# Encoder layer on one core: the convolution group normalised two tiles a unit, two attention pairs' values a unit later, and a first transfer of 656 columns

## The chip, the cores and the metric

One core of a Trainium2 chip runs the whole layer; the other cores are unused. The metric is device time in microseconds (us). TensorE (PE) multiplies matrices, VectorE (DVE) and ScalarE (ACT) do elementwise work, GpSimd (POOL) and SyncE (SP) here mostly issue DMAs.

## The reference, cut to what matters

512 positions, 2048 channels, float32. The change lies in the first half of the layer, up to the shared output projection.

```python
xn = rms_norm(x, attn_norm_g[l])
proj = jnp.einsum("bsd,dc->bsc", xn, w_in[l])
u_val, u_gate, q, k, v = jnp.split(proj, split_pts, axis=-1)
y_conv = conformer_conv(u_val, u_gate, ...)   # GLU, depthwise conv of 31, layer_norm over 1024 channels, silu
y_na = neighborhood_attention(heads(q), heads(k), heads(v), rpb[l])
mixed = concat([rms_norm(y_conv, conv_out_g[l]), rms_norm(y_na, na_out_g[l])])
x = x + jnp.einsum("bsc,cd->bsd", mixed, w_out[l])
# then a gated MLP with a depthwise conv of 3, and a last rms_norm
```

## The kernel before

**Units.** Channels lie on the partitions, positions along the free axis. Every product is taken in two parts for precision: an operand is split into a rounded part and the rest (`whi`, `wlo` for weights; `xh`, `xl` for the input; `mah`, `mal` for the normalised convolution group; `mbh`, `mbl` for the attention group). A *unit* is one weight tile of 128x1024: DMA to `raw`, ACT rounds it to `whi` (L129), DVE subtracts to `wlo` (L130), and `group` (L142) issues 24 matmuls of 128x512: sixteen with `whi`, alternately on L146 and L147, then eight with `wlo` on L149. Four `whi` and four `wlo` tiles exist (`NW = 4`), so the `whi` of a unit can be written once the unit four before it has used its own.

**The order.** `ORDER` (L63) sets the projections: `a` is a convolution tile (gate and value), `V` the values, `q` one pair of heads (a q projection of two units and a k projection of two). After the projections `out_half` (L676) multiplies the convolution group (`ma`) by its half of the output weights, one unit for each of 16 output tiles `po`, then the attention group (`mb`). After each unit `tick` (L154) runs the next step of two generators: `attention` (L542) and, on its own list, `group_a` (L493). What a generator emits between two `yield`s so falls behind one unit; each engine then works its own queue in order.

**Attention.** For each pair of heads one step emits the value products of the pair before (`values`, `po<-pt,v` on L608), the scores (`sc<-k,q`, L562) and the softmax. Three units later (four for pairs 5 and 6, `LATER`) the probabilities are transposed on PE (`trp`, L588) and ACT copies them out of PSUM as `pt` (L597); the next step's `values` needs these copies.

**The convolution group.** `group_a` waits for the last tap, sums the eight `y` tiles, subtracts the mean, squares, takes the root `rln` in `roots_of_sums` (L271), and then, for eight tiles at a stretch: multiply by `rln` (DVE, L517), Silu (ACT, L518) and `split` (L208), which makes `mah` on ACT (L211) and `mal` on DVE (L212). The squares of all eight tiles (ACT L217 and L220, sums on DVE L221) stand behind that, with no `yield` in the stretch. `RA_AFTER` yields later the second root `ra` is taken; `read_a` (L691) needs it before it can read an output tile of the first half out of PSUM (`oa<-po,ra`, L696).

**PSUM.** The pool `psm` has three banks of 128x512, used in turn by each q or k projection `pj`, by one half of each `values`, and by each output tile `po`. A bank is free again when its reader is done: DVE's `q<-pj` or `k<-pj` (L536), DVE's `ao` addition (L617), or DVE's `oa<-po,ra`. The column sums `st` use the bank of the other half of `values`.

**The start.** Eight matmuls on ones (`WARM`, L117) run while the first data come. The input comes in four rows of 512 columns, each with 384 columns of weights for the first three projections and 16 of gains, in one transfer `xw` (L318). For row 0 ACT and DVE split x (L328, L330, L333) and the weights (L329 the first 128 columns, L331 the other 256); the first matmuls are on L455.

Of the kernel before, what the change touches and what calls it, by code (L numbers as in the profile page):

```python
# [10 lines left out]
F32 = mybir.dt.float32  # L11
F32R = mybir.dt.float32r
AF = mybir.ActivationFunctionType
ALU = mybir.AluOpType
AX = mybir.AxisListType

P = 128
D = 2048
S = 512
# [11 lines left out]
KD = D // P  # L31
NC_ = CONV // P
# [15 lines left out]
AHEAD = 3  # L48
FAR = 8
NW = 4  # L50
WARM = 8
ROWS = 4
SOONER = 100
TAPS = 4
# [7 lines left out]
ROW = 2048  # L62
ORDER = "aaaaaaVVaqaqqqqqqq"  # L63
LATER = (5, 6)
RA_AFTER = 5

PCOLS = [("g1", KD), ("dww", NC_ * CK), ("dwb", NC_), ("lng", NC_), ("lnb", NC_), ("cog", NC_),
         ("nag", NC_), ("g2", KD), ("fww", 2 * NF * 3), ("fwb", 2 * NF)]
# [9 lines left out]
def layer(ctx: ExitStack, tc: tile.TileContext, xT, xg, xn, xw, w_0, w_in, w_v, w_out, w_up, w_down, par, tab, g3, out):  # L78
    nc = tc.nc
# [16 lines left out]
    def t2(name, dt=F32):  # L96
        return tp.tile([P, S], dt, tag="t2k", name=name)

    def t4(shape, name):

        return wpool.tile(shape, F32, tag="raw", name=name, bufs=NR)

    prm = consts.tile([P, NPAR], F32, name="prm")
    g1 = consts.tile([P, KD], F32, name="g1")

    def pc(name, i):
        o = POFF[name] + i
        return prm[:, o:o + 1]
# [6 lines left out]
    ps = psm.tile([P, S], F32, tag="mm", name="warm")  # L115
    for _ in range(WARM):
        nc.tensor.matmul(ps[:, :P], ones, ones, start=True, stop=True)  # L117
# [3 lines left out]
    def raw_unit(src, n):  # L121
        raw = t4([P, U * P], "raw")
        return raw, nc.sync.dma_start(raw[:, :n], src)
# [81 lines left out]
        if job:  # L205
            open_job.append(job)

    def split(src, g, name):  # L208

        h, l = t2(name + "h", F32R), t2(name + "l", F32R)  # L210
        nc.scalar.activation(h, src, AF.Copy, scale=g)  # L211
        nc.vector.scalar_tensor_tensor(l, src, g, h.bitcast(F32), op0=ALU.mult, op1=ALU.subtract)  # L212
        return h, l

    def sum_sq(acc, src, first, to=slice(0, S)):
        if first:
            nc.scalar.activation(acc, src, AF.Square)  # L217
        else:
            q = t2("sq")[:, to]
            nc.scalar.activation(q, src, AF.Square)  # L220
            nc.vector.tensor_add(acc, acc, q)  # L221
# [35 lines left out]
    def halved(src):  # L257

        h, l = t2("ah", F32R), t2("al", F32R)
        nc.scalar.activation(h, src, AF.Copy)  # L260
        nc.vector.tensor_sub(l, src, h.bitcast(F32))
        return h, l

    def column_sums(two):

        ps = stat()
        for i in range(2):
            nc.tensor.matmul(ps, ones_r, two[i], start=i == 0, stop=i == 1)
        return ps

    def roots_of_sums(acc, n, name, wait=1):  # L271

# [12 lines left out]

    xs, x1 = [], []
    pin = tc.keep_in_program_order

    def split_x(k, x, g=None):
        h, l = t2("xh", F32R), t2("xl", F32R)  # L290
        g = (g1 if g is None else g)[:, k:k + 1]
        pin(nc.scalar.activation(h, x, AF.Copy, scale=g))
        pin(nc.vector.scalar_tensor_tensor(l, x, g, h.bitcast(F32), op0=ALU.mult, op1=ALU.subtract))
        xs.append((h, l))
# [18 lines left out]
    todo = [(t, i) for t in range(S // P) for i in range(2)]  # L313
    for k in range(ROWS):
        n = 3 * P
        both = t4([P, S + n + KD], "xw")
        m = S + n + (0 if k else KD)
        pin(nc.sync.dma_start(both[:, :m], xw[k][:, :m]))  # L318
        x, raw, lo = both[:, :S], both[:, S:S + n], t2("wel", F32R)[:, :n]
        if k:  # L320
            split_x(k, x)
            his = [t2("weh", F32R)[:, :n]]
            pin(nc.scalar.activation(his[0], raw, AF.Copy))
        else:
            his = [t2("weh", F32R)[:, :P], t2("weh", F32R)[:, P:n]]
            h, l = t2("xh", F32R), t2("xl", F32R)
            g = both[:, S + n:S + n + 1]
            pin(nc.scalar.activation(h[:, :H], x[:, :H], AF.Copy, scale=g))  # L328
            pin(nc.vector.tensor_copy(his[0], raw[:, :P]))  # L329
            pin(nc.vector.tensor_scalar(h[:, H:], x[:, H:], g, None, op0=ALU.mult))  # L330
            pin(nc.scalar.activation(his[1], raw[:, P:], AF.Copy))  # L331
            pin(nc.vector.tensor_copy(g1, both[:, S + n:]))
            pin(nc.vector.scalar_tensor_tensor(l, x, g, h.bitcast(F32), op0=ALU.mult, op1=ALU.subtract))  # L333
            xs.append((h, l))
        o = 0
        for h in his:
            to = slice(o, o + h.shape[-1])
            pin(nc.vector.tensor_sub(lo[:, to], raw[:, to], h.bitcast(F32)))
            o = to.stop
        pieces.append((k, k + 1, his, lo))  # L340
    for p in range(ROWS // 2, KD // 2):
        x = t4([P, 2 * S], "x")
# [6 lines left out]
    for u in range(2):  # L349
        raw, i = raw_unit(w_in[1, :, u * U * P:(u + 1) * U * P], U * P)  # L350
# [8 lines left out]
    for step in ORDER:  # L359
# [5 lines left out]
        i = next(a_ if step == "a" else q_)  # L365
# [69 lines left out]
    ys, ypair, gate = [], [], []  # L435
# [55 lines left out]
    ma, ra = [], []  # L491

    def group_a():  # L493
        yield
        while taps:
            yield
        acc = t2("acc")
        nc.vector.tensor_add(acc, ys[0], ys[1])
        for i in range(2, NC_):
            nc.vector.tensor_add(acc, acc, ys[i])  # L500
        two = halved(acc)
        yield
        yield
        ps = column_sums(two)
        mu = t2("mu")
        nc.vector.tensor_scalar(mu, ps, 1.0 / CONV, None, op0=ALU.mult)
        acc = t2("acc")
        for i in range(NC_):
            nc.vector.tensor_sub(ys[i], ys[i], mu)
            sum_sq(acc, ys[i], i == 0)  # L510
        yield
        yield
        yield
        r = yield from roots_of_sums(acc, CONV, "rln")
        acc = t2("acc")
        for i in range(NC_):
            nc.vector.tensor_mul(ys[i], ys[i], r)  # L517
            nc.scalar.activation(ys[i], ys[i], AF.Silu, scale=pc("lng", i), bias=pc("lnb", i))  # L518
            ma.append(split(ys[i], pc("cog", i), "ma"))
        for i in range(NC_):  # L520
            sum_sq(acc, ys[i], i == 0)
        for _ in range(RA_AFTER):
            yield

        ra.append((yield from roots_of_sums(acc, CONV, "ra")))

# [15 lines left out]
    def attention():  # L542


        def banks(name):
            two = psa.tile([P, 2, S], F32, tag="sc", name=name)
            return [two[:, j, :2 * SLOTS] for j in range(2)] + [
                psa.tile([P, 2 * SLOTS], F32, tag="tr", name=name, bufs=2) for _ in range(2)]
# [65 lines left out]
        def taken(p, po):  # L614
            ao = t2("ao")
            nc.scalar.activation(grid(ao), blocks(po[0]), AF.Copy)
            nc.vector.tensor_add(grid(ao), grid(ao), blocks(po[1]))  # L617
            mb.append(split(ao, pc("nag", p), "mb"))
            sum_sq(acc_na, ao, p == 0)

        pts = None
        for p in range(NP_ + 1):
            while len(qks) < min(p + 1, NP_):
                yield
            if p < NP_:
                tabs = [t4([P, 2, 2 * SLOTS], "tab") for _ in QUADS]
                for n, tb in enumerate(tabs):
                    nc.sync.dma_start(tb, tab[2 * p:2 * p + 2, :, n * 2 * SLOTS:(n + 1) * 2 * SLOTS]
                                      .rearrange("h p k -> p h k"))
            yield  # L630
            if p:
                po = [psa.tile([P, S], F32, tag="po", name="po"), psm.tile([P, S], F32, tag="mm", name="po")]
                values(p - 1, pts, po)
            if p < NP_:
                four = banks("sc")
                for n, quad in enumerate(QUADS):
                    scores(*qks[p], quad, four[2 * n:][:2], p or n)
            if p:
                taken(p - 1, po)
            if p == NP_:  # L640
                return
# [426 lines left out]
    a = four(True)  # L1068
# [30 lines left out]
def _cols(a):  # L1099

    return np.asarray(a).reshape(-1, P).T
# [70 lines left out]
```

## Time and profile before

| | us |
|---|---|
| runs of the kernel, median of 3 | 1961.98 (1961.77 to 1962.09) |
| the profiled execution | 1962.36 |
| its span, first to last instruction | 1960.4 |
| PE busy in the span | 1938.6 |
| DVE busy in the span | 1611.0 |
| ACT busy in the span | 1083.8 |

In the rows below, a line of the timeline gives start, duration, engine, line of the kernel, operation, what it writes and reads, and in brackets the idle time of the engine ahead of it with what ended that. A row with "x8" stands for eight instructions in a row, and its duration runs from the first's start to the last's end. PEclk is the granted TensorE clock as a share of full speed.

### The profile page before, as it was taken

Reading aid. Unit: us, or ns where it says so; the run is one execution under the profiler, and the core shown is the slowest. Engines: PE = TensorE matmul, PEld = TensorE weight load, DVE = VectorE, ACT = ScalarE, POOL = GpSimd, SP = SyncE. Lnnn points to the kernel's source line nnn. Section 1 sums busy time; section 2 is a strip of 40 time slices with the busy share of each in tenths; the row PEclk is TensorE's granted clock in tenths of the full one; section 3 lists DMA queues with packets and bytes.
Section 4 is the critical chain, followed back from the end, with each engine's and each line's share of the span. In section 5 each row is a group of like instructions: output and inputs, shape, how many; then the busy total and the mean of one; then the engine's idle time right before and its main releaser. Section 6 shows DMA issues by size and latency. Waiting matters only on the chain.

```text
span 1960.4 us, 27992 instructions
## 1 busy us (share of the span) xinstructions
PE 1938.6 (99%) x10327; PEld 1652.5 (84%) x10327; DVE 1611.0 (82%) x2310; ACT 1083.8 (55%) x1725; POOL 226.3 (12%) x310
## 2 busy tenths in 40 slices
PE   9999999979999999999999999999999999999998
PEld 8888888868888888888888888888888888888886
DVE  5999878975657898888888888888889898885764
ACT  7222233576526666666666666666666644554654
POOL 0111111100011111111111111111110300000000
PEclk9999999999999999999999999999999999999999
DMA  9676667767758899999999999999995967666553
GB/s 372 179 194 178 190 182 189 194 167 218 251 151 215 212 250 253 270 243 271 241 270 244 270 247 265 262 249 263 249 257 166 386 239 236 216 215 194 192 201 121
DMA packets 141529, 448.89 MB, mean 229 GB/s; under 512 B 14928, under 2 KB 27216, under 8 KB 139984
## 3 DMA queue, kind: packets, MB, share of 16 engines
q1 hardware_dynamic: 89168, 291.90, 43.1%
q0 software_dynamic: 42624, 148.92, 35.1%
q10 hardware_dynamic: 9600, 6.29, 1.1%
q8 instruction: 81, 1.33, 0.3%
q14 instruction: 56, 0.46, 0.1%
HBM read 428.17 MB, written 111.15 MB: 275 GB/s over the span
## 4 chain that ended last, share of the span: by engine, by line
PE 97%; ACT 1%; DVE 1%; issue 0%; ACTq 0%
PE pu L823 44%; PE pd L962 21%; PE pj L146 5%; PE pj L147 5%; PE pj L149 5%; PE pv L417 4%; PE po L146 3%; PE po L147 3%; PE po L149 3%; PE pj L455 1%; PE po L608 1%; PE pj L459 1%; PE sc L562 1%; PE trp L588 0%; PE trx L718 0%; ACT y L518 0%
## 5 line engine op out<-in xcount | busy, mean ns | idle before, releaser
L129 ACT ACTIVATE whi<-raw 128x1024 fp32r<-128x1024 f32 (+1 forms) x574 | 604.1, 1055 | 550.6 <-PE pd L962 116.0
L130 DVE TENSOR_TENSOR wlo<-raw,whi 128x1024 fp32r<-128x1024 f32 (+1 forms) x574 | 698.6, 1218 | 214.8 <-ACT whi L129 186.5
L823 PE MATMUL pu<-xc,whi 128*128 128x512 f32 x2464 | 593.1, 391 | 0.0
L823 PEld LDWEIGHTS pu<-xc,whi 128*128 128x128 f32 x2464 | 451.4, 188 | 86.8 <-DVE xc L711 0.4
L823 PEld LDWEIGHTS pu<-xc,wlo 128*128 128x128 f32 x2464 | 319.4, 191 | 13.7
L823 PE MATMUL pu<-xc,wlo 128*128 128x256 f32 x2464 | 324.3, 283 | 0.0
L962 PE MATMUL pd<-whi,ho 128*128 128x512 f32 x1232 | 305.1, 389 | 0.0
L962 PEld LDWEIGHTS pd<-whi,ho 128*128 128x128 f32 x1232 | 231.1, 188 | 48.7 <-DVE vl L836 0.5
L146 PE MATMUL pj<-xh,whi 128*128 128x512 f32 x464 | 182.0, 392 | 0.0
L485 DVE SCALAR_TENSOR_TENSOR y<-ch,prm,y 128x500 f32<-128x500 f32 (+14 forms) x240 | 176.9, 741 | 5.4
L147 PE MATMUL pj<-xl,whi 128*128 128x512 f32 x464 | 180.6, 389 | 0.0
L962 PE MATMUL pd<-wlo,ho 128*128 128x512 f32 x616 | 165.1, 389 | 0.0
L962 PEld LDWEIGHTS pd<-wlo,ho 128*128 128x128 f32 x616 | 115.6, 188 | 24.0
L832 ACT ACTIVATE pu<-pu 128x512 f32<-128x512 f32 x132 | 76.6, 580 | 92.0 <-PE pu L823 92.0
L772 POOL DMA_DIRECT2D raw<-in_w_up x88 | 78.6, 893 | 351.5 <-DVE wlo L130 160.8
L203 POOL DMA_DIRECT2D ws<-in_w_down x88 | 79.9, 907 | 316.7 <-DMA ws<-in_w_down 126.5
L149 PE MATMUL pj<-xh,wlo 128*128 128x512 f32 x464 | 114.6, 389 | 0.0
L146 PEld LDWEIGHTS pj<-xh,whi 128*128 128x128 f32 x464 | 87.1, 188 | 19.5 <-issue 1.6
L149 PEld LDWEIGHTS pj<-xh,wlo 128*128 128x128 f32 x464 | 87.1, 188 | 18.1
L147 PEld LDWEIGHTS pj<-xl,whi 128*128 128x128 f32 x464 | 87.1, 188 | 17.8
L200 POOL DMA_DIRECT2D ws<-ws x44 | 23.3, 530 | 317.5 <-PE pj L149 102.9
L200 POOL DMA_DIRECT2D ws<-in_w_down x44 | 23.4, 531 | 298.5 <-PE pj L149 125.9
(215 smaller groups left out, 2109.2 us busy)
## 6 DMA issues: line engine op xcount, KB each, us to landing
raw<-in_w_up SPq DMA_DIRECT2D x220, 512.0 KB, 5.9
ws<-in_w_down POOLq DMA_DIRECT2D x132, 512.0 KB, 6.5
raw<-in_w_up POOLq DMA_DIRECT2D x88, 512.0 KB, 7.4
raw<-ws SPq DMA_DIRECT2D x88, 512.0 KB, 3.3
raw<-in_w_down SPq DMA_DIRECT2D x66, 512.0 KB, 3.8
raw<-in_w_in SPq DMA_DIRECT2D x58, 512.0 KB, 5.3
ws<-ws POOLq DMA_DIRECT2D x44, 512.0 KB, 5.5
raw<-in_w_out SPq DMA_DIRECT2D x32, 512.0 KB, 4.9
```

The lines of the kernel that those rows point to most:

```text
L129: i = nc.scalar.activation(hi[:, :n], raw[:, :n], AF.Copy)
L130: j = nc.vector.tensor_sub(lo[:, :n], raw[:, :n], hi[:, :n].bitcast(F32))
L146: nc.tensor.matmul(ps, hi, mh, start=first and k == 0, stop=False)
L147: nc.tensor.matmul(ps, hi, ml, start=False, stop=False)
L149: i = nc.tensor.matmul(ps, lo[:, wk * P:(wk + 1) * P], mh, start=False, stop=last and k == len(ws) - 1)
L203: nc.gpsimd.dma_start(wsum[c][k], w_down[k, {1: A21, 2: A11, 4: A11, 6: A12}[c]], accum_op=ALU.add, max_dma_last_dim=ROW)
L417: m = nc.tensor.matmul(banks[c], xs[2 * u + k][x][:, c * P:(c + 1) * P], w[l][:, k * S:(k + 1) * S], start=u == x == l == k == 0, stop=las ...
L485: nc.vector.scalar_tensor_tensor(y[:, a:b], h[:, a + j - PAD:b + j - PAD], prm[:, o:o + 1], y[:, a:b], op0=ALU.mult, op1=ALU.add)
L772: nc.gpsimd.dma_start(a[c], w_up[f, q2], accum_op=ALU.add)
L823: i = nc.tensor.matmul(ps[:, :n], part[:, k * P:(k + 1) * P], comb[c][k][:, :n], start=j == 0 and not more, stop=j == 2 * U - 1, skip_grou ...
L832: nc.scalar.activation(to, ps, AF.Copy)
L962: m = nc.tensor.matmul(ps[i], h[:, o + t * P:o + (t + 1) * P], w[:, d], start=start and not more and kind == 0 and j == 0, stop=stop and k ...
```

## The change

- `group_a`: a `yield` after every third tile in the loop that subtracts the mean (one of three plain yields behind it stays). In the loop of the normalisation each tile's square follows its split at once, a `yield` stands after every second tile, and the `RA_AFTER` yields are gone. So the eight tiles fall behind four units.
- `split(..., vector=True)`: for the convolution group the rounded part `mah` is made on DVE (a `tensor_scalar`) and no longer on ACT.
- `SLOW = (4, 5)`: one more `yield` ahead of the step that holds the values of pairs 4 and 5. Since the generator goes on from there, everything of the attention behind it moves one unit, then two.
- The start: the first transfer holds x, 128 columns of weights and the gains (656 columns); the other 256 weight columns of row 0 go to a tile `wer` by a second transfer. Rows 1 to 3 are transferred as before. `WARM` is 7.

```diff
-WARM = 8
+WARM = 7
-RA_AFTER = 5
+SLOW = (4, 5)
...
-    def split(src, g, name):
+    def split(src, g, name, vector=False):
...
-        nc.scalar.activation(h, src, AF.Copy, scale=g)
+        if vector:
+            nc.vector.tensor_scalar(h, src, g, None, op0=ALU.mult)
+        else:
+            nc.scalar.activation(h, src, AF.Copy, scale=g)
         nc.vector.scalar_tensor_tensor(l, src, g, h.bitcast(F32), op0=ALU.mult, op1=ALU.subtract)
...
-        both = t4([P, S + n + KD], "xw")
-        m = S + n + (0 if k else KD)
+        both = t4([P, S + n], "xw")
+        m = S + (n if k else P + KD)
         pin(nc.sync.dma_start(both[:, :m], xw[k][:, :m]))
...
         else:
+            raw = [both[:, S:S + P], t2("wer")[:, :n - P]]
+            pin(nc.sync.dma_start(raw[1], xw[k][:, m:]))
             his = [t2("weh", F32R)[:, :P], t2("weh", F32R)[:, P:n]]
...
         for i in range(NC_):
             nc.vector.tensor_sub(ys[i], ys[i], mu)
             sum_sq(acc, ys[i], i == 0)
-        yield
-        yield
+            if i % 3 == 2:
+                yield
         yield
         r = yield from roots_of_sums(acc, CONV, "rln")
         acc = t2("acc")
         for i in range(NC_):
             nc.vector.tensor_mul(ys[i], ys[i], r)
             nc.scalar.activation(ys[i], ys[i], AF.Silu, scale=pc("lng", i), bias=pc("lnb", i))
-            ma.append(split(ys[i], pc("cog", i), "ma"))
-        for i in range(NC_):
+            ma.append(split(ys[i], pc("cog", i), "ma", True))
             sum_sq(acc, ys[i], i == 0)
-        for _ in range(RA_AFTER):
-            yield
+            if i % 2 == 1:
+                yield
...
             while len(qks) < min(p + 1, NP_):
+                yield
+            if p - 1 in SLOW:
                 yield
```

What this does to ACT's queue behind the root `rln`, where the copies `pt` of pair 4 (counted from 0) stand. Before:

```order
L281 ACTIVATE r<-rln 128x512 x2
L518 ACT_TABLE_LOAD
L518 ACTIVATE y<-y,prm 128x512 x2
L211 ACTIVATE mah<-y,prm 128x512
L518 ACTIVATE y<-y,prm 128x512
L211 ACTIVATE mah<-y,prm 128x512
L518 ACTIVATE y<-y,prm 128x512
L211 ACTIVATE mah<-y,prm 128x512
L518 ACTIVATE y<-y,prm 128x512
L211 ACTIVATE mah<-y,prm 128x512
```

```order
L211 ACTIVATE mah<-y,prm 128x512 x2
L217 ACTIVATE acc<-y 128x512
L220 ACTIVATE sq<-y 128x512 x7
L597 ACTIVATE pt<-trp 128x384 x4
L129 ACTIVATE whi<-raw 128x1024 x2
L616 ACTIVATE ao<-po 128x8x8x8
```

Now, in the numbers of the changed file's lines (Silu L523, squares L220 and L223, `pt` L601):

```order
L523 ACT_TABLE_LOAD
L523 ACTIVATE y<-y,prm 128x512 x3
L220 ACTIVATE acc<-y 128x512
L523 ACTIVATE y<-y,prm 128x512 x2
L223 ACTIVATE sq<-y 128x512
L601 ACTIVATE pt<-trp 128x384 x4
L129 ACTIVATE whi<-raw 128x1024
L223 ACTIVATE sq<-y 128x512
L523 ACTIVATE y<-y,prm 128x512
L129 ACTIVATE whi<-raw 128x1024 x2
L223 ACTIVATE sq<-y 128x512
L523 ACTIVATE y<-y,prm 128x512 x2
```

Ahead of `pt` stood eight Silus, eight `mah` and eight squares; now five Silus and two squares, and no `mah`.

DVE's queue behind `rln`, up to the reads of PSUM that free PE's banks. Before:

```order
L283 TENSOR_SCALAR rln<-r,rln 128x512
L517 TENSOR_TENSOR y<-y,rln 128x512 x8
L212 TENSOR_SCALAR mal<-y,prm,mah 128x512 x8
L221 TENSOR_TENSOR acc<-acc,sq 128x512 x4
L536 TENSOR_TENSOR k<-pj,rstd_545 128x512
L221 TENSOR_TENSOR acc<-acc,sq 128x512 x3
L130 TENSOR_TENSOR wlo<-raw,whi 128x1024 x2
L617 TENSOR_TENSOR ao<-ao,po 128x8x8x8
```

Now, the end of the same stretch (`mah` L212, `mal` L215, sums of squares L224, reads of q and k L540, `ao` L621):

```order
L130 TENSOR_TENSOR wlo<-raw,whi 128x1024
L224 TENSOR_TENSOR acc<-acc,sq 128x512
L212 TENSOR_SCALAR mah<-y,prm 128x512
L130 TENSOR_TENSOR wlo<-raw,whi 128x1024
L215 TENSOR_SCALAR mal<-y,prm,mah 128x512
L224 TENSOR_TENSOR acc<-acc,sq 128x512
L212 TENSOR_SCALAR mah<-y,prm 128x512
L215 TENSOR_SCALAR mal<-y,prm,mah 128x512
L224 TENSOR_TENSOR acc<-acc,sq 128x512
L540 TENSOR_TENSOR q<-pj,rstd_546 128x512
L621 TENSOR_TENSOR ao<-ao,po 128x8x8x8
```

From `rln` to `q<-pj` DVE now has eight `y`, six `mah`, six `mal`, five sums `acc`, `k<-pj`, three `wlo` and `q<-pj`; the last two tiles' `mah` and `mal` follow behind the next scores. On PE two units, where there was one, now stand between the transposes and the value products of pair 4, and again for pair 5, where the second of them is the first unit of the output projection.

More of the change, by code (lines that the diff above doesn't have):

```diff
@@ L315, in layer @@
         n = 3 * P
-        both = t4([P, S + n + KD], "xw")
-        m = S + n + (0 if k else KD)
+        both = t4([P, S + n], "xw")
+        m = S + (n if k else P + KD)
         pin(nc.sync.dma_start(both[:, :m], xw[k][:, :m]))
-        x, raw, lo = both[:, :S], both[:, S:S + n], t2("wel", F32R)[:, :n]
+        x, raw, lo = both[:, :S], [both[:, S:m]], t2("wel", F32R)[:, :n]
         if k:
@@ L322, in layer @@
             his = [t2("weh", F32R)[:, :n]]
-            pin(nc.scalar.activation(his[0], raw, AF.Copy))
+            pin(nc.scalar.activation(his[0], raw[0], AF.Copy))
         else:
+            raw = [both[:, S:S + P], t2("wer")[:, :n - P]]
+            pin(nc.sync.dma_start(raw[1], xw[k][:, m:]))
             his = [t2("weh", F32R)[:, :P], t2("weh", F32R)[:, P:n]]
             h, l = t2("xh", F32R), t2("xl", F32R)
-            g = both[:, S + n:S + n + 1]
+            g = both[:, S + P:S + P + 1]
             pin(nc.scalar.activation(h[:, :H], x[:, :H], AF.Copy, scale=g))
-            pin(nc.vector.tensor_copy(his[0], raw[:, :P]))
+            pin(nc.vector.tensor_copy(his[0], raw[0]))
             pin(nc.vector.tensor_scalar(h[:, H:], x[:, H:], g, None, op0=ALU.mult))
-            pin(nc.scalar.activation(his[1], raw[:, P:], AF.Copy))
-            pin(nc.vector.tensor_copy(g1, both[:, S + n:]))
+            pin(nc.scalar.activation(his[1], raw[1], AF.Copy))
+            pin(nc.vector.tensor_copy(g1, both[:, S + P:m]))
             pin(nc.vector.scalar_tensor_tensor(l, x, g, h.bitcast(F32), op0=ALU.mult, op1=ALU.subtract))
@@ L335, in layer @@
         o = 0
-        for h in his:
+        for r, h in zip(raw, his):
             to = slice(o, o + h.shape[-1])
-            pin(nc.vector.tensor_sub(lo[:, to], raw[:, to], h.bitcast(F32)))
+            pin(nc.vector.tensor_sub(lo[:, to], r, h.bitcast(F32)))
             o = to.stop
@@ L1121 @@
     w_0 = np.ascontiguousarray(np.stack([w_in[i].reshape(P, KD, P) for i in (NC_, 0, NC_ + 1)], 2)).reshape(P, -1)
-    xw = np.stack([np.concatenate([xg[k // 2][:, k % 2 * S:(k % 2 + 1) * S], w_0[:, 3 * k * P:3 * (k + 1) * P],
-                                   _cols(a["attn_norm_g"][0])], axis=1) for k in range(ROWS)])
+    xw = []
+    for k in range(ROWS):
+        w, g = w_0[:, 3 * k * P:3 * (k + 1) * P], _cols(a["attn_norm_g"][0])
+        xw.append(np.concatenate([xg[k // 2][:, k % 2 * S:(k % 2 + 1) * S]]
+                                 + ([w, g] if k else [w[:, :P], g, w[:, P:]]), axis=1))
+    xw = np.stack(xw)
     wo = a["w_out"][0]
```

## The prediction

> **What bounds the kernel now.** I read the page first, then who waited for whom on PE, then the timeline round the one long wait.
>
> ```profile
> span 1960.4 us, 27992 instructions
> PE 1938.6 (99%) x10327; PEld 1652.5 (84%) x10327; DVE 1611.0 (82%) x2310; ACT 1083.8 (55%) x1725; POOL 226.3 (12%) x310
> PE 97%; ACT 1%; DVE 1%; issue 0%; ACTq 0%
> PE po L608 <- ACT pt L597: 12.7, 1, 12.7
> PE warm L117 <- DVE ones L112: 1.1, 1, 1.1
> 1939.94 12.47 PE pd L962 x54
> ```
>
> PE is 97% of the chain that ended last. In the whole span it waits twice: 1.1 us at the start, and once 12.7 us for ACT's `pt`. Its last matmul in the chain ends at 1952.4, 8.0 before the span's end: 1.1 + 12.7 + 8.0 is all of 1960.4 - 1938.6. So only what shortens that wait, the start, or adds a new PE wait, can move the time. ACT's timeline there:
>
> ```profile
> 426.25 1.52 ACT L518 ACTIVATE y<-y,prm 128x512 f32<-128x512 f32 x2 [0.91 <-DVE y L517]
> 427.68 0.71 ACT L211 ACTIVATE mah<-y,prm 128x512 fp32r<-128x512 f32 x1
> 435.59 1.32 ACT L211 ACTIVATE mah<-y,prm 128x512 fp32r<-128x512 f32 x2
> 437.33 3.73 ACT L220 ACTIVATE sq<-y 128x512 f32<-128x512 f32 x7
> 440.97 1.59 ACT L597 ACTIVATE pt<-trp 128x384 f32<-128x384 f32 x4
> 442.45 2.00 ACT L129 ACTIVATE whi<-raw 128x1024 fp32r<-128x1024 f32 x2
> ```
>
> PE had left the transposes by 424.21 (next rows), but ACT first worked through Silu, `mah` and squares of eight tiles, from 426.25 to 440.97. PE's timeline, its chain, and two windows:
>
> ```profile
> 424.21 0.48 PE L146 MATMUL pj<-xh,whi 128*128 128x512 f32 x1
> 442.61 2.62 PE L608 MATMUL po<-pt,v 64*64 64x64 f32 x48 [12.70 <-ACT pt L597]
> 452.66 0.39 PE L146 MATMUL pj<-xh,whi 128*128 128x512 f32 x1
> 456.45 1.81 PE pj L149 x8
> 461.89 1.81 PE pj L149 x8
> 475.92 1.37 PE po L608 x38
> 478.65 0.43 PE pj L146
> 442.60:446.00 3.40, 3.39 (x64) 3.17 (x66) 3.30 (x4) 2.45 (x3) 0.00 (x0) 0.50 0.78 271
> 458.00:470.00 12.00, 12.00 (x60) 10.04 (x59) 4.18 (x4) 3.13 (x6) 2.17 (x3) 1.00 0.73 199
> ```
>
> A unit is 461.89 - 456.45 = 5.44 us; values and scores without a wait are 478.65 - 475.92 = 2.73 us. After the wait the granted clock is 0.50 (the last but two number of a window's row) and the same values and scores take 447.1 - 442.6 = 4.5. From the unit that begins at 424.21 to the one at 452.66 lie unit, values and scores, unit: 5.44 + 2.73 + 5.44 = 13.61, and they took 28.45. **The stall is worth 14.8 us**, 12.7 of waiting and some 2 of slow rows.
>
> **The change part by part.** *The old wait.* PE now has the unit at 424.2 and one more, so it reaches the values at 424.21 + 10.88 = 435.1. ACT starts at 426.25 (DVE's `y` sets that, unchanged). Five Silus at 0.70 apart (two take 1.52 with 0.1 of overlap), two squares at 0.53 (3.73 for seven) and the four copies, 1.5, end at 426.25 + 3.5 + 1.1 + 1.5 = 432.4. `pt` is 2.7 us early: all 14.8 us go, unless something else is late.
>
> *What is late next: DVE.* PE continues with values and scores to 437.8 and a unit to 424.21 + 3 x 5.44 + 2.73 = 443.3. The unit behind that writes the PSUM bank of the last q projection, and `q<-pj` stands at the end of DVE's row of the change. DVE's prices:
>
> ```profile
> 425.53 4.90 DVE L517 TENSOR_TENSOR y<-y,rln 128x512 f32<-128x512 f32 x8
> 430.35 2.78 DVE L212 SCALAR_TENSOR_TENSOR mal<-y,prm,mah 128x512 fp32r<-128x512 f32 x4
> 443.76 2.35 DVE L130 TENSOR_TENSOR wlo<-raw,whi 128x1024 fp32r<-128x1024 f32 x2
> L996 DVE TENSOR_SCALAR g<-g 128x512 f32<-128x512 f32 x2 | 0.8, 422 | 1.0 <-DMA g<-in_g 1.0
> L483 DVE TENSOR_SCALAR y<-ch,prm 128x512 f32<-128x512 f32 x8 | 4.3, 541 | 0.0
> ```
>
> Start to start, a two-tensor operation of 512 takes 0.60 (eight `y` from 425.53 to 430.35), `mal` 0.68, a `wlo` 1.14. From 425.53: eight `y` 4.8, six `mal` 4.1, five sums 3.0, `k` and `q` 1.2, three `wlo` 3.4, together 16.5. No row has `mah` on DVE: between L996, whose scalar is a constant, and L483, with two scalars from a tile; less 0.07 that neighbours overlap, 0.35 to 0.47. I take 0.43; the upper bound is a two-tensor price, 0.60. Six are 2.6 (2.1 to 3.6), so `q` is read at 425.5 + 19.1 = 444.6 and **PE waits 1.4 us** (0.9 to 2.4). Behind `q<-pj` on DVE stand `ao` and the next softmax, which ACT's exponentials wait for.
>
> [...]
>
> *The second root.* `ra` is now taken earlier: its column sum `st<-ah` stands inside a unit, behind fifteen matmuls, in the third unit after 444.65. PE gets there at 444.65 + 10.88 + 15 x 0.227 = 458.9. ACT makes `ah` behind the softmax of pair 5, the last squares and two `whi`:
>
> ```profile
> 446.03 0.68 DVE L617 TENSOR_TENSOR ao<-ao,po 128x512 f32<-128x512 f32 x1
> 451.56 0.68 DVE L536 TENSOR_TENSOR q<-pj,rstd 128x512 f32<-128x512 f32 x1
> 487.19 1.48 ACT L580 ACTIVATE s<-s,su 128x192 f32<-128x192 f32 x4
> L577 ACT ACTIVATE s<-s,nm 128x192 f32<-128x192 f32 x64 | 28.3, 442 | 14.8 <-DVE nm L574 14.8
> 538.86 0.63 ACT L260 ACTIVATE ah<-accna 128x512 fp32r<-128x512 f32 x1 [0.90 <-DVE accna L221]
> ```
>
> Before, DVE needed 5.53 us from `ao` to the end of the last scores' scaling. From 444.6 that is 450.15; a `mah` and a `wlo` stand next, so the first reciprocal comes at 451.7. From there ACT has eight copies at 0.35, four exponentials at 0.44, two squares at 0.53, two `whi` at 0.95 and `ah` 0.63: 8.2 us, 459.9. **PE waits 1.0 us** (0 if ACT slips ahead, 2 if DVE's reciprocals are late too). With `st` the unit's end moves; the next transposes find their probabilities done, the last copies being ahead of those two `whi`.
>
> *Banks of the output projection.* Its second unit starts behind values and scores; its fourth needs `oa<-po,ra` of the first. In DVE's queue ahead of that stands a sum `accna` that waits for an ACT square, behind a `whi` that waits for the second unit's last `whi` matmul. From that unit's start: 3.63 + 0.95 + 0.53, then sum, two maxima, two scalings and `oa`, some 3.1: 8.2, against 10.88 for two units. Covered by 2.7 us; without it PE would stand for the rest. The weights' DMAs are issued a unit or more earlier than needed, as DVE's `wlo` releases their `raw` tiles; nothing there ends last.
>
> *The start.*
>
> ```profile
> 0.75 1.80 SPq L318 DMA_DIRECT2D xw<-in_xw  x4
> 4.07 0.51 ACT L328 ACTIVATE xh<-xw 128x256 fp32r<-128x256 f32 x1 [1.83 <-DMA xw<-in_xw]
> 4.71 1.48 PE L455 MATMUL pj<-xh,weh 128*128 128x512 f32 x3
> 6.03 0.87 PE L455 MATMUL pj<-xl,weh 128*128 128x512 f32 x3
> 6.73 0.85 PE L459 MATMUL pj<-xh,wel 128*128 128x512 f32 x3
> 5.26 0.72 ACT L292 ACTIVATE xh<-xw,g 128x512 fp32r<-128x512 f32 x1 [0.38 <-DMA xw<-in_xw]
> 5.89 0.51 ACT L323 ACTIVATE weh<-xw 128x384 fp32r<-128x384 f32 x1
> 7.42 0.85 PE L455 MATMUL pj<-xh,weh 128*128 128x512 f32 x3
> 5.00:10.00 5.00, 5.00 (x21) 4.11 (x21) 4.59 (x9) 4.09 (x8) 0.00 (x0) 1.00 1.01 373
> ```
>
> The transfer is issued at 0.75 and used at 4.07. It loses 256 x 4 x 128 bytes, 0.131 MB; at the 373 GB/s of the window that is 0.35 us, if its rate sets the landing. The first three matmuls are 0.44 apart (6.03 - 4.71), the next ones 0.23: if that pace changes at a fixed time, 0.35 sooner saves 0.35 x 0.23 / 0.44 = 0.18; if it moves along, 0.35. I take **0.2 gained**. One warm-up matmul less ends the warm-up with the earlier data, nothing else. The second matmul needs the other weights, by the same bytes landed at about 4.07; bounded by row 1, which ACT began at 5.26, they would come 1.2 late and PE would lose 0.9. Row 1's later issue (0.45, a quarter of the four issues' 1.80) is inside the 1.0 us between its weights (6.40) and their use (7.42).
>
> *Sum.* 14.8 - 1.4 - 1.0 + 0.2 = 12.6. The profiled execution took 1962.36 with a span of 1960.4; less 12.6, 1949.8 and 1947.8. It lies 0.38 above the median of the runs, so the median should be **1949.4**.
>
> **The rivals.** *No new wait.* If ACT and DVE run a little tighter, as both bounds allow, 14.8 + 0.35 come off: 1946.8. Against it: DVE has few pauses between 425.5 and 443.8 already, and gets six `mah` more.
>
> *DVE late enough to slow the clock.* With `mah` at 0.60, the wait for `q` is 2.4; add a late operand, and the granted clock falls as after the old wait, for another 2 us of slow rows: 14.8 - 2.4 - 1.0 - 2.0 + 0.2 = 9.6, or 1952.4. For it: the 0.50 above. Against: that stood after 12.7 us.
>
> [...]
>
> *Slower than before.* The circle above, PE to `whi` on ACT to `accna` on DVE to PE's bank, closes if DVE is over 2.7 us late there. It stands in the three passes of values inside the output projection; each could then cost one unit, 16.3 in all: with the two small waits 1962.0 - 14.8 - 0.2 + 2.4 + 16.3 = 1965.7. Against it: DVE would have to find no slack again in 50 us, and its idle share rises from 458 on (4.18 busy in 12).
>
> *The stall merely moves*, the copies `pt` or `oa` being as late as before: 1962. Against it are the 2.7 us twice.
>
> **How the numbers follow.** The sum 0.77, no new wait 0.09, slow clock 0.09, slower 0.03, moved 0.02. The likeliest's own range, from its bounds: 14.8 - 0.9 - 0 + 0.35 gives 1947.7, and 14.8 - 2.4 - 2.0 - 0.9 gives 1952.5. The range takes in the two nearest rivals: 1946.8 to 1953.0. Within 0.2% (3.9 us), about what can be told from no change here, is only the moved stall: 0.02; slower 0.03; faster 0.95.
>
> **What would show it.** PE's list of waits without the 12.7 us for `pt`, in its place a wait for DVE's `q` of 1 to 2.5 us near 444 and one for ACT's `ah` near 459; `mah` on DVE at 420 to 540 ns; no window at a clock of 0.50 there; the first data used near 3.7. It is wrong if PE waits over 3 us anywhere before 600, if `mah` costs over 0.7, or if `wer` lands later than row 1 did.

## The result, and the profile after

| | before | changed |
|---|---|---|
| median of the runs, us | 1962.03 (1961.77 to 1962.73, 4 runs) | 1951.08 (1951.02 to 1951.12, 4 runs) |
| profiled execution, its span | 1962.36, 1960.4 | 1951.12, 1949.3 |

The change is faster by 10.95 us: ratio 0.9944, 95% interval 0.9926 to 0.9961. Forecast were 1949.4 and a span of 1947.8; of the 12.6 us expected, the spans show 11.1.

PE's list of waits in the changed kernel, the whole span, has no `pt` any more:

```profile
PE warm L117 <- DVE ones L112: 1.1, 1, 1.1
PE pj L146 <- DVE q L540: 1.0, 1, 1.0
PE pj L460 <- ACT weh L326: 0.9, 1, 0.9
PE st L271 <- ACT ah L263: 0.6, 1, 0.6
```

The middle, from the changed kernel's timelines, its groups by form and one window:

```profile
425.03 0.48 PE L146 MATMUL pj<-xh,whi 128*128 128x512 f32 x1
426.34 3.10 DVE L522 TENSOR_TENSOR y<-y,rln 128x512 f32<-128x512 f32 x5
431.66 1.59 ACT L601 ACTIVATE pt<-trp 128x384 f32<-128x384 f32 x4
436.10 1.45 PE L612 MATMUL po<-pt,v 64*64 64x64 f32 x48
444.79 0.68 DVE L540 TENSOR_TENSOR q<-pj,rstd 128x512 f32<-128x512 f32 x1
445.61 0.47 PE L146 MATMUL pj<-xh,whi 128*128 128x512 f32 x1 [1.04 <-DVE q L540]
460.77 0.50 PE L271 MATMUL st<-ah,ones 128*128 128x512 f32 x1 [0.59 <-ACT ah L263]
661.65 0.94 PE L818 MATMUL pu<-xc 128*128 128x512 f32 x3
L212 DVE TENSOR_SCALAR mah<-y,prm 128x512 fp32r<-128x512 f32 x8 | 3.8, 478 | 0.0
446.00:458.00 12.00, 12.00 (x55) 9.89 (x54) 9.38 (x22) 9.77 (x29) 1.41 (x2) 1.00 0.78 252
```

ACT's copies end at 433.25 and PE comes for them at 436.10, two units and 0.2 after 425.03; they are 2.85 us early. The next two waits stand where they were forecast. The clock is 1.00 where it had been 0.50. The row that begins at 424.21 before begins at 425.03 now; the first `pu` of the up projection stood here before:

```profile
673.15 0.94 PE L812 MATMUL pu<-xc 128*128 128x512 f32 x3
```

From that row to `pu` were 673.15 - 424.21 = 248.94 us and are 236.62: the middle gained 12.3. But PE enters it 0.82 late. The start, from the changed kernel's timeline:

```profile
0.75 0.39 SPq L321 DMA_DIRECT2D xw<-in_xw  x1
1.19 0.42 SPq L329 DMA_DIRECT2D wer<-in_xw  x1
1.66 1.37 SPq L321 DMA_DIRECT2D xw<-in_xw  x3
3.73 0.51 ACT L333 ACTIVATE xh<-xw 128x256 fp32r<-128x256 f32 x1 [1.49 <-DMA xw<-in_xw]
4.14 0.40 ACT L336 ACTIVATE weh<-wer 128x256 fp32r<-128x256 f32 x1
4.36 1.42 PE L460 MATMUL pj<-xh,weh 128*128 128x512 f32 x3
6.91 0.72 ACT L295 ACTIVATE xh<-xw,g 128x512 fp32r<-128x512 f32 x1 [2.37 <-DMA xw<-in_xw]
8.10 0.72 PE L460 MATMUL pj<-xh,weh 128*128 128x512 f32 x2 [0.93 <-ACT weh L326]
```

The first matmul is 0.35 sooner, and `wer` causes no wait. Row 1, issued 0.45 later than before, is split at 6.91, where it had been split at 5.26: PE waits for it, and everything behind is late. The last 0.4 of the difference lies behind PE's last matmul: from the start of ACT's last operation to the span's end go 5.6 us before and 6.0 after. The change touches nothing there. Yet the stretch is 5.6 to 5.7 in the six profiles of this study with all `mah` on ACT, and 5.8 to 6.0 in the eight with all or most of them on DVE; why stays open.

### The profile page after: what moved, and what is told of

It reads as the page before. It is cut to its first block, busy times and chain, and to the rows that moved or that the text cites. A ratio compares the mean times of both kernels' runs of the same rounds, so it can differ in the third digit from the quotient of the medians.

```text
span 1949.3 us, 27981 instructions
## 1 busy us (share of the span) xinstructions
PE 1937.2 (99%) x10325; PEld 1650.3 (85%) x10325; DVE 1613.0 (83%) x2318; ACT 1078.3 (55%) x1717; POOL 225.7 (12%) x310
## 4 chain that ended last, share of the span: by engine, by line
PE 96%; DVE 2%; ACT 1%; DMA 1%; issue 0%; SPq 0%; ACTq 0%; DVEq 0%
PE pu L829 44%; PE pd L968 21%; PE pj L149 5%; PE pj L146 5%; PE pj L147 5%; PE pv L422 4%; PE po L146 3%; PE po L147 3%; PE po L149 3%; PE pj L460 1%; PE pj L464 1%; PE po L612 0%; PE trp L592 0%; PE sc L566 0%; PE trx L724 0%
```

## The experiments

All kernels in one table. "Unit" is the start of PE's first matmul behind the transposes of pair 4 (424.21 before); ahead of it PE waits only in the first product, so it carries the start. "To `pu`" is the time from there to the first `pu`, and carries the middle. Waits are those behind the first matmul. The kernel before took 1962.03 to 1962.78 in the four sets of runs, so each median stands beside that of the kernel before on the same chip.

| kernel | median | before there | span | unit | to `pu` | PE waits for |
|---|---|---|---|---|---|---|
| before | 1962.03 | | 1960.4 | 424.21 | 248.94 | `pt` 12.7 |
| changed | 1951.08 | 1962.03 | 1949.3 | 425.03 | 236.62 | q 1.0, `weh` 0.9, `ah` 0.6 |
| `after_again` | 1951.29 | 1962.56 | 1949.5 | 425.21 | 236.69 | q 1.1, `ah` 0.6, `weh` 0.5 |
| `mid_only` | 1950.31 | 1962.78 | 1948.8 | 424.44 | 236.66 | q 1.1, `ah` 0.6 |
| `start_only` | 1963.42 | 1962.78 | 1961.4 | 425.08 | 248.64 | `pt` 12.7, `weh` 0.7, `xc` 0.2 |
| `wer_second` | 1953.04 | 1962.78 | 1951.2 | 426.83 | 236.69 | `wer` 1.5, q 1.1, `ah` 0.6 |
| `wer_act` | 1949.91 | 1962.78 | 1947.9 | 423.54 | 236.76 | q 1.2, `ah` 0.6 |
| `wer_wide` | 1951.05 | 1962.56 | 1949.8 | 425.38 | 236.65 | q 1.1, `ah` 0.6, `weh` 0.5 |
| `no_slow` | 1953.07 | 1962.65 | 1951.3 | 424.67 | 239.09 | `pt` 2.6, `al` 1.2, `weh` 0.9, `ah` 0.3 |
| `slow_only` | 1949.57 | 1962.65 | 1947.6 | 423.91 | 236.34 | `pt` 1.9 |
| `act_mah` | 1949.70 | 1962.65 | 1947.5 | 424.81 | 235.35 | `weh` 1.2, `ah` 0.6 |
| `best` | 1948.60 | 1962.65 | 1946.2 | 423.56 | 235.06 | `ah` 0.3 |
| `lean` | 1948.75 | 1962.56 | 1946.7 | 423.90 | 235.41 | `ah` 0.6 |
| `slow_act` | 1950.01 | 1962.56 | 1949.0 | 423.74 | 238.02 | `pt` 1.9 |

### The start

`mid_only`: the change without its start.

```diff
-WARM = 7
+WARM = 8
...
-        both = t4([P, S + n], "xw")
-        m = S + (n if k else P + KD)
+        both = t4([P, S + n + KD], "xw")
+        m = S + n + (0 if k else KD)
...
-            pin(nc.sync.dma_start(raw[1], xw[k][:, m:]))
```

> The change without its start: one first transfer of 912 columns and eight warm-up matmuls, as before; the convolution group and the later values as changed. Theory (row 1 of the first product lands late because of the new start, and PE loses 0.8 us by it for good): the span is 0.8 to 0.9 us shorter than with the whole change, 1948.4 to 1948.5, the time near 1950.2; the row 1 split on ACT begins at 5.3 again, no PE wait for `weh`. Rival (the new start is worth its 0.2, and the 0.8 come from the order behind it): the span is 1949.3 or longer. The waits for DVE's q and ACT's `ah`, 1.0 and 0.6 us, stay in both.

`start_only`: the other half, the new start put into the kernel before.

```diff
-WARM = 8
+WARM = 7
...
-        m = S + n + (0 if k else KD)
+        m = S + (n if k else P + KD)
...
+            pin(nc.sync.dma_start(raw[1], xw[k][:, m:]))
```

> The kernel before with the new start alone (656 columns first, the other two tiles' weights as a second transfer, seven warm-up matmuls). Theory: the first matmul 0.35 us sooner, row 1's split 1.6 later, a PE wait of 0.9 for `weh`, and in sum the span 0.8 longer than before, 1961.2; the wait for `pt` stays near 12.7. Rival (the prediction's term): 0.2 shorter, 1960.2. A third: the old wait for `pt` swallows the delay, since ACT and DVE were the late ones there, and the span stays 1960.4.

Without its start the change is 12.47 us faster than before by the medians; with it, 10.95 and, in the runs of `after_again`, 11.27. Its profiled span is only 0.5 shorter, in a run whose first data were used at 4.25 (4.07 before); its four spans go from 1948.1 to 1948.9. Put into the kernel before, the start costs 0.64 us by the medians, and PE still waits 12.7 for `pt`: that wait does not swallow it. So the theory holds: the new start loses time. Two of `start_only`'s ten runs took 1970.2 and 1970.3. They count in its ratio (1.0013, 1.0003 to 1.0022), which therefore says more than 0.64 us; the profile is of another run, and what made them stays open.

What holds row 1 up? Three kernels vary the second transfer alone.

`wer_second`:

```diff
+            pin(nc.sync.dma_start(ahead, xw[1][:, :S + n]))
             pin(nc.sync.dma_start(raw[1], xw[k][:, m:]))
```

> The whole change, but row 1's transfer is issued ahead of the second transfer of row 0 (`wer`). Theory (the order of the issues sets who lands first): row 1 lands near 5, `wer` near 5.3 to 5.5 in its place, PE waits some 1.2 us for `wer` in the first row but not for row 1, and the span is 0.3 us shorter than with the whole change. Rival (the transfer of 1024-byte rows stretches what is next to it, whatever the order): row 1 lands at 6.3 or later again, both waits appear, and the span is longer than 1949.3.

`wer_act`:

```diff
-            pin(nc.sync.dma_start(raw[1], xw[k][:, m:]))
+            pin(nc.scalar.dma_start(raw[1], xw[k][:, m:]))
```

> The whole change, but `wer` is issued from ACT's queue, so that SP issues row 1 0.45 us sooner, at 1.2 as before. Theory A (issue time alone): row 1 lands 0.45 sooner, at 6.4, the PE wait shrinks from 0.9 to 0.5. Theory B (row 1 was behind `wer` in one queue): row 1 lands by 5.3 and PE does not wait for `weh`; the span is 0.8 to 1.0 shorter, 1948.3 to 1948.5. Theory C (the bytes in flight at that time, not the queue): landing stays at 6.7 to 6.9 and the span at 1949.3.

`wer_wide`:

```diff
-            raw = [both[:, S:S + P], t2("wer")[:, :n - P]]
-            pin(nc.sync.dma_start(raw[1], xw[k][:, m:]))
+            raw = [both[:, S:S + P], t2("wer")]
+            pin(nc.sync.dma_start(raw[1], xw[k][:, m + n - P - S:])); raw[1] = raw[1][:, S + P - n:]
```

> The whole change, but the second transfer brings 512 columns a row instead of 256 (2048 bytes, the last 1024 of them used), on SP as before. It tells what in the queue holds row 1 up. Theory D (the short rows of 1024 bytes): packets of 2048 bytes do not upset the queue, row 1 lands 0.35 us later than its bytes alone would (0.131 MB more at 373 GB/s), by 5.7, and PE's wait for `weh` goes; span 1948.3 to 1949.0. Theory E (any further transfer between the two on this queue): row 1 lands at 6.8 to 7.2 again and the wait is 0.9 to 1.3; span 1949.3 to 1949.7.

The timeline of `wer_act`, ACT and PE:

```profile
1.05 0.42 ACTq L329 DMA_DIRECT2D wer<-in_xw  x1
4.03 0.40 ACT L336 ACTIVATE weh<-wer 128x256 fp32r<-128x256 f32 x1
5.19 0.72 ACT L295 ACTIVATE xh<-xw,g 128x512 fp32r<-128x512 f32 x1 [0.76 <-DVE wel L343]
6.53 0.86 PE L460 MATMUL pj<-xh,weh 128*128 128x512 f32 x3
```

With `wer` in ACT's queue row 1 is there by 5.19, the wait is gone, and the first product runs through: theory B. A later issue alone (A) would have left it at 6.4. The same stretch, 4.40 to 6.00, in windows (the last two numbers are the DMA engines' mean busy share and GB/s): before, changed, `wer_act`.

```profile
4.40:6.00 1.60, 1.60 (x6) 1.32 (x5) 1.53 (x5) 1.22 (x4) 0.00 (x0) 1.00 1.07 367
```

```profile
4.40:6.00 1.60, 1.60 (x6) 1.36 (x6) 1.22 (x3) 0.14 (x1) 0.00 (x0) 1.00 0.88 186
```

```profile
4.40:6.00 1.60, 1.60 (x8) 1.14 (x8) 1.17 (x4) 0.84 (x3) 0.00 (x0) 1.00 1.01 354
```

In the changed kernel the engines are busy 0.88 of the time and move half the bytes, in 96 packets of 0.23 us on the mean where there were 193 of 0.14: the packets in hand take longer, rather than nothing having been issued. The bytes asked for are the same in `wer_act`, so theory C falls too, as far as row 1 goes. Wider rows do not help (`wer_wide`, ACT's timeline):

```profile
4.35 0.42 ACT L336 ACTIVATE weh<-wer 128x256 fp32r<-128x256 f32 x1
7.26 0.72 ACT L295 ACTIVATE xh<-xw,g 128x512 fp32r<-128x512 f32 x1 [2.49 <-DMA xw<-in_xw]
```

That is theory E: row 1 is used at 7.26 although the rows are 2048 bytes. In all six kernels with `wer` between the two on SP's queue row 1 is split at 6.6 to 7.3, in the seven that keep it off that queue or have none at 5.2 to 5.6. In `wer_second` the hole falls on `wer`, now behind row 1:

```profile
6.52 0.73 PE L460 MATMUL pj<-xh,weh 128*128 128x512 f32 x2 [1.51 <-ACT weh L336]
7.79 1.01 PE L464 MATMUL pj<-xh,wel 128*128 128x512 f32 x2
```

Neither of its two theories gave that: `wer` is used at 6.05, not 5.4, and the row behind it runs slow, which is taken up below. ACT's queue does not always do away with the hole either. In `wer_act` it falls on row 2, and in `slow_act`, which has the same transfers, too (at 7.44, after 1.10):

```profile
7.48 0.73 ACT L295 ACTIVATE xh<-xw,g 128x512 fp32r<-128x512 f32 x1 [1.15 <-DMA xw<-in_xw]
```

In `best` and `lean`, again with the same transfers, row 2 is split at 6.42 and 6.72 without such a wait. PE came to row 2 late enough not to wait in any of the four. So the delay came with the further transfer, and in each run that showed it the first to be late was the third transfer of SP's queue: row 1, `wer` or row 2. With `wer` on ACT's queue it no longer reached row 1; what makes it stays open.

### The middle

`no_slow`:

```diff
-SLOW = (4, 5)
+SLOW = ()
```

> The whole change without its later values (SLOW empty): PE reaches the values of pair 4 one unit, 5.44 us, sooner, at 430.5 in the time of the changed kernel's profile, while ACT's `pt` still end at 433.2. Theory (the interleaved group brings most of the old wait, the later values the rest): PE waits 2.8 us for `pt` there, and the span is 1.5 to 2.8 longer than with the whole change, as the waits for q and `ah` may fall away. A wait of 2.8 tests the clock from below: if only long waits slow it (12.7 did), it stays 1.00; if any wait of a few us does, a window at 0.50 follows and some 2 us more are lost. Rival (the interleaving alone is enough and the later values cost or bring nothing): no wait for `pt` over 0.5, span within 0.5 of the whole change.

`slow_only`, against the kernel before:

```diff
+SLOW = (4, 5)
...
+            if p - 1 in SLOW:
+                yield
             if p < NP_:
```

> The kernel before with the later values alone: the values of pairs 4 and 5 one unit later, the convolution group as before, `mah` on ACT. Theory: `pt` still end near 442.6, PE comes one unit later, at 435.1, and waits 12.7 - 5.44 = 7.3 us; the span is 5.4 shorter than before. The clock falls to 0.50 behind this wait too, as it did behind 12.7, so that the some 2 us of slow rows stay. Rival (the wait moves to another place, as every step behind comes later too): the span is shorter by less than 3. If the clock stays 1.00 behind 7.3 us, the span is 7 to 7.5 shorter.

`act_mah`:

```diff
-            ma.append(split(ys[i], pc("cog", i), "ma", True))
+            ma.append(split(ys[i], pc("cog", i), "ma"))
```

> The whole change, but all `mah` stay on ACT. Theory (the two engines exchange places): two `mah` at 0.7 ahead of `pt` end these at 434.6, still 1.3 ahead of PE, so no wait for `pt`; q is read no sooner than in the whole change, as DVE now waits for ACT's `mah` instead of making them, so its wait stays 0.5 to 1.0; two `mah` more behind the softmax make `ah` 1.4 later and its wait 1.5 to 2.5. In sum the span is 0.5 to 2 us longer than with the whole change. Rival (DVE's own work sets the read of q, as the prediction had it): six `mah` at 0.40 less on DVE, q read 2.4 sooner, no wait for q, and the span shorter by up to 1 if `ah` is not later.

`no_slow` did as its theory said: a wait of 2.6 for `pt`, and the clock stayed 1.00 behind it. The interleaving, with `mah` on DVE, therefore takes 248.94 - 239.09 = 9.85 us out of the middle without the later values.

`slow_only` gained more than any theory of it gave, 12.6 us in the middle. PE's timeline and ACT's copies there:

```profile
440.70 1.59 ACT L597 ACTIVATE pt<-trp 128x384 f32<-128x384 f32 x4
442.35 1.44 PE L608 MATMUL po<-pt,v 64*64 64x64 f32 x48 [1.85 <-ACT pt L597]
```

The expectation's arithmetic of the wait was right and its reading of the edit wrong. `pt` ended near 442.3, as expected. But PE's row of this program has three units between transposes and values, where it had one; the added `yield` asks for one more, and why the order came out with two stays open. (In the changed kernel the same `yield` added one.) So PE came two units later: 12.7 - 10.88 = 1.8, and 1.85 was measured.

`act_mah` refuted its theory and upheld the rival. DVE reads q 4.15 us sooner than in the changed kernel (at 444.79 there):

```profile
440.64 0.68 DVE L540 TENSOR_TENSOR q<-pj,rstd 128x512 f32<-128x512 f32 x1
```

PE does not wait for it, and the middle is 236.62 - 235.35 = 1.27 us shorter. It was DVE's own work that made q late, as the prediction had it. But the rival expected 2.4, six `mah`. In DVE's row of this program the order changed as well: two `wlo` and one sum that stood ahead of q, some 2.9 us, now stand behind it, while DVE idles 1.3 us there for ACT. So the run does not part the price of `mah` from that of the order that comes with it. Put together, later values alone, by two units, take 12.6 us out of the middle; the interleaving, `mah` left on ACT and the values one unit later, ends another 236.34 - 235.35 = 1.0 below; moving `mah` to DVE, with its order, gives 1.3 back.

### Together

`best`:

```diff
-            pin(nc.sync.dma_start(raw[1], xw[k][:, m:]))
+            pin(nc.scalar.dma_start(raw[1], xw[k][:, m:]))
...
-            ma.append(split(ys[i], pc("cog", i), "ma", True))
+            ma.append(split(ys[i], pc("cog", i), "ma", i > 2))
...
-            nc.vector.tensor_mul(got[-1], ps, rstd[0])
+            with shifted(-SOONER * (p == 6 and j == 0)): nc.vector.tensor_mul(got[-1], ps, rstd[0])
```

> The whole change with `wer` issued from ACT's queue, the first three tiles' `mah` on ACT, the other five on DVE, and the read of the q projection of pair 6 ahead on DVE's queue (of one sum and one `wlo`). Theory (the wait for q is DVE's work ahead of the read): three `mah` at 0.40, a sum at 0.60 and a `wlo` at 1.14 less stand ahead of it, 2.9 in all, so the wait of 1.2 goes; two `mah` more ahead of `pt` leave these 1.3 ahead of PE; the wait for `ah` stays 0 to 0.6. The span is 1.2 to 1.8 shorter than with `wer` on ACT alone (1947.9): 1946.1 to 1946.7. Rival (ACT is now the late one): `pt` or the weights' `whi` come late, a new PE wait of 1 us or more appears between 425 and 465, and the span is 1947.9 or longer.

`lean`, the edits of `wer_act` and `act_mah` in one kernel:

> The whole change with `wer` issued from ACT's queue and all `mah` left on ACT; interleaving and later values as changed. Theory (the two losses are independent: 1.2 us for `weh` by the queue, the q wait by the `mah` on DVE): the span is 1.2 shorter than with `mah` on ACT alone (1947.5), 1946.3, and 2.5 to 3 shorter than the whole change on the same chip; the only wait left behind the start is the 0.6 for `ah`. Rival (both losses hide one behind the other): 1947.3 or longer.

`after_again`, the changed kernel on the same chip:

> The whole change once more, unedited, beside the other three on one chip. Every theory here expects its own span again, 1949.3 give or take the 0.8 by which starts have differed between runs, with the waits for q (1.0), `weh` (0.9) and `ah` (0.6).

`slow_act`, the kernel before with `SLOW`, the new start and `nc.scalar` for `wer`:

> The kernel before with the later values and with the new start, `wer` issued from ACT's queue; the convolution group not interleaved, `mah` on ACT. Theory (start and middle add up): the span is 0.4 to 0.6 shorter than with the later values alone (1947.6), 1947.0 to 1947.2, with the wait of 1.9 for `pt` and no other behind the start. Rival (the wait for `pt` grows by what the start saves, since ACT and DVE set it): 1947.6.

The waits of `best` behind the start, all of them:

```profile
PE st L271 <- ACT ah L263: 0.3, 1, 0.3
```

`best` did as its theory said: q is no longer waited for, and the span is 1946.2. It takes 1948.60 where the kernel before takes 1962.65 (ratio 0.9930, 0.9914 to 0.9947), `lean` 1948.75 against 1962.56 (0.9929, 0.9914 to 0.9944), and the changed kernel beside `lean` 1951.29. Both beat both kernels. `lean` did not quite reach its theory's span: 1946.7 instead of 1946.3, 0.8 below `act_mah` instead of 1.2, still below the rival's 1947.3. `lean` needs two small edits, so it is the one to keep; no run tells the two apart. `slow_only`, a single `yield` more than the kernel before, is already 13.08 us faster than it by the medians, where the whole change is 10.95.

`slow_act` failed its theory in the profiled execution: its span is 1.4 longer than that of `slow_only`, though it starts 0.17 sooner and waits the same. Its other three spans, 1947.1, 1947.8 and 1947.9, lie nearer to the forecast, 1947.0 to 1947.2. PE's timeline behind that wait:

```profile
442.17 2.58 PE L610 MATMUL po<-pt,v 64*64 64x64 f32 x48 [1.85 <-ACT pt L599]
444.52 2.11 PE L564 MATMUL sc<-k,q 64*64 64x192 f32 x36
446.56 0.50 PE L146 MATMUL pj<-xh,whi 128*128 128x512 f32 x1
```

Values and scores take 446.56 - 442.17 = 4.39 instead of 2.72 (442.35 to 445.07 in `slow_only`): 1.67 lost at the same wait. The granted clock, in windows cut where its record changes; PE's busy time, count and clock. `slow_act`:

```profile
438.86:442.27 3.41, 1.56 (x11) 1.00 0.78 241
442.27:445.68 3.41, 3.41 (x64) 0.50 1.05 329
445.68:449.10 3.42, 3.42 (x39) 1.00 1.08 306
```

`slow_only`, cut on the same raster of 3.41 us, which begins elsewhere in each run:

```profile
438.55:441.97 3.42, 1.94 (x9) 1.00 0.81 228
441.97:445.38 3.41, 3.04 (x85) 1.00 0.98 317
```

The wait of 1.85 us lies in one window of `slow_act`, and the next was granted half the clock, 0.50. In `slow_only` the border falls into the wait (idle 1.48, then 0.37), and the clock stayed 1.00. `no_slow` and `wer_second` the same way:

```profile
427.91:431.33 3.42, 2.47 (x11) 1.00 0.07 5
431.33:434.74 3.41, 1.79 (x64) 1.00 1.08 219
```

```profile
4.41:7.82 3.41, 1.77 (x8) 1.00 0.96 282
7.82:11.23 3.41, 3.41 (x10) 0.50 1.03 419
```

A wait of 2.57, split into 0.95 and 1.62, left the clock at 1.00; one of 1.5 with 0.1 of other idling, 1.64 in one window, was followed by 0.50. The count of matmuls in `wer_second`'s slow window is 10 where the next holds 17; seven at 0.227 make about 1.6 us of its 1.8 later unit. (One of that kernel's four executions took some 1.7 us less than the profiled one, which would fit such a window missing; no trace shows it.)

Idle time within a window did not settle it alone, though. In `start_only` PE's last matmul ends at 1953.23, and the window is idle for 3.41 - 1.52 = 1.89, but the next was granted 1.00:

```profile
1951.71:1955.12 3.41, 1.52 (x7) 1.00 0.81 268
1955.12:1958.53 3.41, 0.00 (x0) 1.00 0.78 263
```

What else counts is open.

## Why the prediction was right, and where it was not

*The old wait.* Right to the step: `pt` early by 2.85 (forecast 2.7), all of the stall gone, the slow rows too. ACT, DVE and PE all came 0.8 to 1.0 later than forecast, with the start, so the distance between them held. The profile before could not show that the change does this twice over: by the later values without the interleaving, or by the interleaving without the later values, most of it goes.

*What is late next: DVE.* Right. The read of q was forecast to be done at 444.6, 19.1 behind DVE's first `y`. It starts at 444.79 and, at 0.60, is done by 445.39, 19.05 behind the first `y`, which had moved from 425.53 to 426.34. PE waits 1.04; its unit begins 1.5 later than three units, values and scores behind 425.03 would put it, against 1.4. `mah` stands 0.39 ahead of its neighbour in DVE's timeline, inside 0.35 to 0.47. `act_mah` agrees: with less work on DVE ahead of q the wait is gone.

*The second root.* PE waits 0.59 for `ah`, some 0.9 from start to start, against 1.0. *Banks of the output projection:* no wait, as forecast.

*The start.* This term failed: +0.2 forecast, -0.8 measured, two thirds of the 1.5 us by which the span was missed. The step was "Row 1's later issue (0.45, a quarter of the four issues' 1.80) is inside the 1.0 us between its weights (6.40) and their use (7.42)". It moved row 1's landing by its issue. The runs show row 1 used 1.65 later (5.26 to 6.91) when a further transfer stood ahead of it on the same queue; the bound of a `wer` landing 1.2 late looked at the wrong transfer. Without that the start would have brought about what was forecast. With `wer` on ACT's queue the unit begins at 423.5 to 423.9 in four kernels, with the old start at 423.9 to 424.4 in three, a gain of 0.5 between the means. But more than half of this is luck. The trace's record of the clock begins, with 1.00, at a border of the raster of 3.41 us; ahead of it the first matmuls stand some 0.43 apart, behind it 0.23. `best` and `lean` have the same start and the same first matmul, but their records begin at 4.78 and at 5.49:

```profile
4.49 1.07 PE L460 MATMUL pj<-xh,weh 128*128 128x512 f32 x3
4.49 1.40 PE L460 MATMUL pj<-xh,weh 128*128 128x512 f32 x3
```

Their units begin 0.34 apart (423.56 and 423.90), half the distance of the borders. On the mean the record begins at 4.97 in the four kernels and at 5.72 in the three, and half of the 0.75 between them is 0.37. The first matmul is 0.42 sooner on the mean, and half of that, 0.21, is the start's own gain: the 0.18 that the prediction gave for a pace that changes at a fixed time. The borders also tell why `weh` costs PE 0.9 in the changed kernel (5.42) and 0.5 in `after_again` (6.72) and `wer_wide` (6.98), where the slow pace brought PE to it later; and they may be what `lean` (5.49, against 4.26 in `wer_act`) lacks of its forecast.

*The sum.* 1.0 of the shortfall is the start, 0.1 the middle, 0.4 the end of the last output, which no term covered. The range held the time.

*The rivals.* "No new wait" did not come in this kernel, but `best` shows it near. "Slow clock" did not come either, but what the prediction set against it, that 0.50 had stood only behind 12.7 us, is a weak reason: 1.85 was enough in `slow_act`. The old stall in the same windows, before:

```profile
429.15:432.56 3.41, 0.77 (x4) 1.00 0.58 97
432.56:435.98 3.42, 0.00 (x0) 0.50 0.32 57
442.80:446.21 3.41, 3.41 (x64) 0.50 0.80 271
446.21:449.62 3.41, 3.41 (x35) 1.00 0.77 278
```

The slow stretch at the old wait, 432.56 to 446.21, is 13.65 us long, and the record of the clock begins 426.67 ahead of it: 4 and 125 times 3.413. In the changed kernel the record begins at 5.42 and changes once, behind the last matmul at 1944.19, 568 times 3.413 later. Where no change stands near, as in `slow_only` and `no_slow`, a border is counted on by that step from the record, an estimate. Windows with 1.64 and 1.85 us of idling were enough for half the clock in the next. A wait for q of 2.4, the upper bound, could have cost the 1.7 of slow rows that `slow_act` lost, or nothing, as the 2.57 of `no_slow`, by where it fell.

## What to carry to other kernels

Price a wait by when PE arrives and when the operand is ready, then ask what else moves with the edit: one `yield` moved the values by two units in the kernel before, and that alone brought more than the whole change. Work moved to another engine to hurry one consumer can make the next one in that engine's queue late: here DVE, with `mah` and the order that came with it, read q 4.15 us later. Try the version without the move. When a transfer is split to start sooner, try its second half on another queue, and look at the transfers behind it, not only at the two halves (row 1 was used at 6.57 to 7.26 here with `wer` ahead of it, at 5.19 to 5.64 with `wer` on ACT's queue). And before a few tenths at the start are called a gain, see where the record of the clock begins in each trace (4.26 to 6.98 here).

## What the runs showed of the hardware

- A further transfer on SP's queue, between the first and the second row, made the second usable at 6.57 to 7.26 in six kernels where it was at 5.26, of which its later issue is 0.45, with rows of 1024 bytes or 2048. From 4.40 to 6.00 the DMA engines were 0.73 to 0.95 busy in these six but moved only 186 to 273 GB/s; with the transfer on ACT's queue, or without it, they moved 329 to 408. On ACT's queue it left the second row alone (5.19 to 5.64), but the third came late in two kernels of four (7.48 and 7.44 instead of 6.42 and 6.72). The cause is open.
- The granted clock changed on a raster of 3.41 us that begins elsewhere in each run: from the record's begin to the first fall go 426.67 us in the kernel before and 1938.77 in the changed one, 125 and 568 times 3.413, and the slow stretch before is 13.65, four times. Idle time of PE of 1.64 or 1.85 us within one window was followed by half the clock in the next; 1.62 and 1.48 were not, even where the whole wait was 2.57, and neither was 1.89 at the end of the matmuls. So the same wait of 1.85 cost 1.67 us more in one kernel than in the other; no single limit of idle time fits all windows.
- At the start the first matmuls stand 0.43 apart up to a border of that raster, which fell between 4.26 and 6.98 in the runs here, and 0.23 behind it. Two kernels with the same start so differed by 0.34 us.
